# Routing logits by token rows, low parts on GpSimd, last columns in three parts, and another side for the branch to fall to

## The chip, the core and the metric

The kernel runs on one core of one Trainium2 chip, as one program. The metric is the device time of one execution in microseconds; before the change its median over three runs is 1008.89 us (1007.74 to 1009.09).

## What is computed

A two-layer block (a hybrid mixer and a convolutional feed-forward network per layer) and then a second block: a mixer and a mixture of experts. There are 256 tokens of 1024 numbers, all in fp32. The change lies in the mixture of experts, which the reference writes as

```python
glog = (t @ wg + bg).astype(f32)
gprob = jax.nn.softmax(glog, axis=-1)
g_onehot = jax.nn.one_hot(jnp.argmax(glog, axis=-1), N_GROUPS, dtype=f32)
...
elog_sel = jnp.einsum('tge,tg->te', elog, g_onehot)
eprob = jax.nn.softmax(elog_sel, axis=-1)
top_p, top_i = lax.top_k(eprob, TOP_K)
top_p = top_p / jnp.sum(top_p, axis=-1, keepdims=True)
...
for e in range(N_EXPERTS):
    hid = jax.nn.silu(t @ w_gate[e]) * (t @ w_up[e])
    y = y + gates[:, e:e + 1] * (hid @ w_down[e])
```

with 4 groups of 4 experts, the best group and its two best experts per token, and 256 hidden columns per expert.

## The kernel before, in words

The program is one long stream per engine. The layers and the second mixer take the first 860 us. `moe` (L1534) follows. Its first part, `route` (L1614), is a generator that treats the two tiles of 128 tokens, t = 0 and 1, one behind the other: it adds the out-projection to the residual rows `x` (L1620), transposes the rows on TensorE into `xr`, splits the rows into a high part `xsh` (cast on ScalarE) and a low part `xsl` (subtraction on VectorE, `split` at L362 and `low` at L354), multiplies with the router's weights `rw` (L1636, logits by columns, in fp32), copies the 20 x 128 logits and transposes them back (L1638, L1640), scales them into `rlog` (L1641), and picks group and experts with one-hot vectors (`onehot`, L1521) until `mem` (L1653) holds the membership. A product with a triangular matrix gives each token's place among the expert's tokens (`pos`, L1665 and L1666), a comparison the selection matrix `sel` (`choose`, L1591), and products with it gather the rows of the experts (`gather`, L1595, products at L1600). `low` cuts the subtraction into PIECES = 4 pieces when its engine is GpSimd. `shares` (L1673), another generator, computes the softmax weights `whl` beside it. A `Weave` (L199) interleaves the generators by the costs that they yield; the framework's scheduler then settles each engine's order from priorities and its own estimate of time.

The experts run as 8 pairs. A pair's up product (`up`, L1731) and down product (`down`, L1761) are fp32 products of 64 slots, two experts at a time in the two halves of TensorE's array (`turn`, L580, keeps their order; products at L583). `flip` (L1753, transposition at L327) turns the hidden rows; the down product is split into `yh` and `yl`, and `scatter` (L1777, products at L1783, additions on VectorE at L1784) brings two pairs at a time back to the rows `x`. Weights come through `fetch` (L1585) on SyncE in tiles of 512 KB into a ring of buffers (`er`, `ew`, `mh`, `ml`, `hres`, `grow`). The last pair is scattered alone, and each finished half of the rows is sent out (L1786) by SyncE and ScalarE.

At the end `values_load` (L1850) reads on every engine whether an expert has more than 64 tokens, and `tc.If` (L1852) runs `rest` (L1826) in that case. With these inputs it is not run. The program's blocks stand in the order kernel, `rest`, other side, end; the other side holds waits alone.

Of the kernel before, what the change touches and what calls it, by code (L numbers as in the profile page):

```python
# [10 lines left out]
F32 = mybir.dt.float32  # L11
# [6 lines left out]
P = 128  # L18
# [230 lines left out]
def emit(ctx, tc, A, out, stop=None, dbg=None):  # L249
# [76 lines left out]
    def tr(o, i):  # L326
        T.transpose(o, i, ident[:i.shape[0], :i.shape[0]])  # L327
# [1193 lines left out]
    def onehot(o, v, idx):  # L1521

        n = v.shape[1]
        m = tmp([P, n], tag="ohm")
        k = tmp([P, n], tag="ohk")
        V.tensor_reduce(m, v, axis=AX.X, op=OP.max)
# [7 lines left out]
    def moe(held, a):  # L1534
# [56 lines left out]
        def choose(t, es, src):  # L1591
            V.tensor_tensor(sel[:, t, es], io1[:, None, :].to_broadcast([P, es.stop - es.start, C]),
                            src[:, es, None].to_broadcast([P, es.stop - es.start, C]), op=OP.is_equal)

# [15 lines left out]

        got = []
        greatest = {}

        def route():  # L1614
            for t in range(NT):
# [15 lines left out]
                r = rsqrt1(ss, 1.0 / D, rows[:, t:t + 1])  # L1631
                split(xsh[:, t], xsl[:, t], x[:, t, :])
                yield (0.9, 0.8)
                p = bank(t)
                for k in range(KT):
                    T.matmul(p[:20, 128:256], rw[:, k, :], xr[:, k, :], start=k == 0, stop=k == KT - 1)  # L1636
                lT = tmp([20, 128], tag="dg")
                (V.tensor_copy if t == 0 else SC.copy)(lT, p[:20, 128:256])  # L1638
                yield (0.9, 0.2)
                tr(p[:, 0:20], lT)  # L1640
                V.scalar_tensor_tensor(rl[:, t], p[:, 0:20], r, small[:, SM_RB:SM_RB + 20], op0=OP.mult, op1=OP.add)  # L1641
# [24 lines left out]
                V.tensor_tensor(pos[:, t], pp, m, op=OP.mult)  # L1666
                choose(t, slice(0, 4), pos[:, t])
                yield (0.3, 0.8)
                if t == 1:
                    gather(0, got, range(KT), 1)  # L1670
                    yield (1.9, 0.1)

        def shares(t):  # L1673

            yield lambda: ("mem", t) in done
            m, z, den = (tmp([P, 1], tag=tag) for tag in ("smx", "smz", "smd"))
# [9 lines left out]
            V.tensor_tensor(z, z, r, op=OP.mult)  # L1686
            yield (0, 1.0)
            V.tensor_tensor_reduce(eo[:, 0], o[:, 0], ep[:, 0], 1.0, 0.0, op0=OP.mult, op1=OP.add, accum_out=den)
# [71 lines left out]

        def down(ah, cuts=(0, 1)):  # L1761
            ys = [bank(4), bank(5)]
            last = None
            ws = [[queue.pop(0) for _ in range(2)] for _ in range(2)]
            yh, yl = (tmp([P, D], F32R, tag=tag, bufs=2) for tag in ("yh", "yl"))
            steps = [(j, n) for j in range(2) for n in range(2)] if cuts else [(j, n) for n in range(2) for j in range(2)]
            for j, n in steps:
                ns = slice(n * 512, (n + 1) * 512)
                for i in range(2):
                    last = turn(last, ys[n][halves[i]], ah[:, j, halves[i]], ws[j][i][:, ns], start=j == 0, stop=j == 1)  # L1770
# [5 lines left out]

        def scatter(gys, banks, last=False):  # L1777
            rows_of = [(q, y) for q, yy in gys for y in yy]
            for i, (n, t) in enumerate((n, t) for n in range(2) for t in range(NT)):
# [4 lines left out]
                V.tensor_tensor(x[:, t, ns], p, x[:, t, ns], op=OP.add)  # L1784
                if last:
                    (nc.scalar if t else nc.sync).dma_start(out[t][:, ns], x[:, t, ns])  # L1786

# [10 lines left out]
        def experts():  # L1798
# [23 lines left out]
            scatter(ys, (3, 6, 7))  # L1822
            ys[:] = [(PAIRS - 1, down(state.pop("ah"), ()))]
            scatter(ys, (0, 1, 2, 3), last=True)

# [15 lines left out]
        for t in range(NT):  # L1841
# [9 lines left out]
                              skip_runtime_bounds_check_because="it is a comparison's 0 or 1")  # L1851
        with tc.If(full > 0):  # L1852
            rest()
# [65 lines left out]
```

## Time and profile before

| | us |
|---|---|
| median of three runs | 1008.89 |
| the profiled execution, its own time | 1010.54 |
| the profiled execution, its span | 1008.7 |
| TensorE (PE) busy | 978.6 (97%) |
| VectorE (DVE) busy | 767.1 (76%) |
| ScalarE (ACT) busy | 538.4 (53%) |
| GpSimd (POOL) busy | 115.2 (11%) |

The granted clock of TensorE is 0.987 of full speed over the span. Times in the rows below count in microseconds from the start of the span. SP is SyncE, which issues most transfers; PEld is TensorE's weight load, and a q behind an engine's name is its sequencer. Ends of matmuls are modelled, so starts are the safer numbers.

### The profile page before, as it was taken

To read this page: it belongs to the slowest core of one execution; us is meant where nothing else is said; L and a number is where in the kernel's file an instruction comes from. 1 tells how busy PE (TensorE), PEld (TensorE's weight loads), DVE (VectorE), ACT (ScalarE), POOL (GpSimd) and SP (SyncE) were. 2 spreads that over 40 slices of the span, in tenths; PEclk is the share of its full clock that TensorE was granted. 3 is DMA by queue.
4 is the path that set the end of the run, shared out by engine and by line. 5 is a ranking of instruction groups with operands and counts; after the bars stand their busy time and mean duration, and the time that the engine had idled before them with its cause. 6 is when DMAs were issued, how large, how long until landed. Compare 5 with 4: busy or idle time off the path is not lost.

```text
span 1008.7 us, 16824 instructions
## 1 busy us (share of the span) xinstructions
PE 978.6 (97%) x6056; PEld 797.8 (79%) x6056; DVE 767.1 (76%) x2004; ACT 538.4 (53%) x1036; POOL 115.2 (11%) x195
## 2 busy tenths in 40 slices
PE   8999999999999999999999999999999799899996
PEld 7888887899999988878888999999888577644432
DVE  6698688798888887986887888888899987612224
ACT  6565346766655576653457665555776434231211
POOL 1510003300000065100024000000510120000000
PEclk9999999999999999999999999999999799999998
DMA  9733025655556546330156555555553116889961
GB/s 337 248 102 105 22 84 167 230 189 179 176 188 188 188 149 206 102 111 22 56 174 230 188 173 184 188 187 187 183 177 125 63 62 245 335 322 408 408 245 45
DMA packets 51966, 181.07 MB, mean 180 GB/s; under 512 B 6274, under 2 KB 7203, under 8 KB 51875
## 3 DMA queue, kind: packets, MB, share of 16 engines
q1 hardware_dynamic: 51298, 179.33, 51.8%
q8 instruction: 49, 0.80, 0.3%
q10 hardware_dynamic: 576, 0.59, 0.2%
q14 instruction: 43, 0.34, 0.1%
HBM read 178.86 MB, written 1.05 MB: 178 GB/s over the span
## 4 chain that ended last, share of the span: by engine, by line
PE 85%; DVE 9%; issue 3%; ACT 2%; POOL 1%; DMA 0%; DVEq 0%; ACTq 0%; POOLq 0%
PE b L413 20%; PE b L414 19%; PE b L415 19%; PE b L583 11%; PE b L327 3%; PE b L901 2%; PE b L876 2%; DVE yc L1259 2%; PE b L1600 2%; PE b L1783 2%; PE b L935 1%; DVE wl L360 1%; PE b L855 1%; DVE cy L744 1%; ACT half L424 1%
## 5 line engine op out<-in xcount | busy, mean ns | idle before, releaser
L391 ACT CAST wh<-wr 128x1024 fp32r<-128x1024 f32 x233 | 243.9, 1050 | 181.7 <-PE b L414 92.0
L360 DVE TENSOR_TENSOR wl<-wr,wh 128x1024 fp32r<-128x1024 f32 x214 | 261.7, 1225 | 59.4 <-ACT wh L391 56.6
L413 PE MATMUL b<-xh,wh 128*128 128x256 f32 x816 | 234.8, 288 | 0.0
L414 PE MATMUL b<-xl,wh 128*128 128x256 f32 x816 | 232.7, 285 | 0.0
L415 PE MATMUL b<-xh,wl 128*128 128x256 f32 x816 | 232.0, 284 | 0.0
L413 PEld LDWEIGHTS b<-xh,wh 128*128 128x128 f32 x816 | 156.2, 191 | 3.5 <-issue 1.6
L414 PEld LDWEIGHTS b<-xl,wh 128*128 128x128 f32 x816 | 156.4, 192 | 1.3
L415 PEld LDWEIGHTS b<-xh,wl 128*128 128x128 f32 x816 | 156.3, 191 | 0.1
L360 POOL TENSOR_TENSOR wl<-wr,wh 128x256 fp32r<-128x256 f32 x80 | 56.8, 749 | 556.6 <-ACT wh L391 550.2
L413 PE MATMUL b<-wh,mh 128*128 128x512 f32 x272 | 108.2, 398 | 0.5 <-ACT mh L364 0.5
L414 PE MATMUL b<-wl,mh 128*128 128x512 f32 x272 | 106.8, 393 | 0.0
L413 PE MATMUL b<-wh,xh 128*128 128x512 f32 x256 | 104.3, 413 | 2.6 <-ACT xh L367 2.6
L415 PE MATMUL b<-wh,ml 128*128 128x512 f32 x272 | 106.3, 392 | 0.0
L415 PE MATMUL b<-wh,xl 128*128 128x512 f32 x256 | 104.0, 407 | 0.0
L414 PE MATMUL b<-wl,xh 128*128 128x512 f32 x256 | 103.0, 402 | 0.4 <-DVE wl L360 0.4
L1093 DVE SCALAR_TENSOR_TENSOR fu<-fq,par,fu 128x255 f32<-128x255 f32 (+1 forms) x144 | 69.0, 479 | 2.1
L413 PEld LDWEIGHTS b<-wh,xh 128*128 128x128 f32 x256 | 49.0, 192 | 14.6 <-ACT xh L367 3.8
L415 PEld LDWEIGHTS b<-wh,ml 128*128 128x128 f32 x272 | 51.1, 188 | 11.2
L413 PEld LDWEIGHTS b<-wh,mh 128*128 128x128 f32 x272 | 51.2, 188 | 10.5 <-ACT mh L364 0.8
L414 PEld LDWEIGHTS b<-wl,mh 128*128 128x128 f32 x272 | 51.3, 189 | 9.1
L415 PEld LDWEIGHTS b<-wh,xl 128*128 128x128 f32 x256 | 48.8, 191 | 11.9 <-DVE xl L368 1.2
L414 PEld LDWEIGHTS b<-wl,xh 128*128 128x128 f32 x256 | 49.2, 192 | 10.0 <-DVE wl L360 0.8
(418 smaller groups left out, 1548.3 us busy)
## 6 DMA issues: line engine op xcount, KB each, us to landing
wr<-in_win SPq DMA_DIRECT2D x78, 512.0 KB, 4.3
wr<-in_up SPq DMA_DIRECT2D x72, 512.0 KB, 3.6
wr<-in_down SPq DMA_DIRECT2D x44, 512.0 KB, 3.5
ew<-in_egu SPq DMA_DIRECT2D x30, 512.0 KB, 9.6
wr<-in_wout SPq DMA_DIRECT2D x24, 512.0 KB, 3.5
er<-in_egu SPq DMA_DIRECT2D x20, 512.0 KB, 9.7
ew<-in_edn SPq DMA_DIRECT2D x18, 512.0 KB, 10.2
wr<-in_uptok SPq DMA_DIRECT2D x16, 512.0 KB, 4.1
```

Of the source, the lines that this page charges most:

```text
L327: T.transpose(o, i, ident[:i.shape[0], :i.shape[0]])
L360: eng.tensor_tensor(l[..., c], src[..., c], h[..., c].bitcast(F32), op=OP.subtract)
L391: heads[:] = [(V.tensor_copy if first else SC.copy)(h, raw).ins]
L413: T.matmul(o, ah, bh, start=start, stop=False)
L414: T.matmul(o, ah, bl, start=False, stop=False)
L415: T.matmul(o, al, bh, start=False, stop=stop)
L583: return T.matmul(o, w, m, **kw).ins
L876: T.matmul(pq[:, u * 64:(u + 1) * 64], atu[:, u, 0, :], tv[:, u, :, 0, :], start=True, stop=True)
L901: T.matmul(pq[:, 256 + u * 64:256 + (u + 1) * 64], RRu[:, u, :], pn[:, u, :], start=True, stop=True)
L1093: V.scalar_tensor_tensor(u[:, d:], p[:, :S - d], cw[:, 2 - d:3 - d], u[:, d:], op0=OP.mult, op1=OP.add)
L1259: V.scalar_tensor_tensor(y, zp[:, ct, j:j + S], cwh[:, 31 * ct + j:31 * ct + j + 1], y, op0=OP.mult, op1=OP.add)
L1600: T.matmul(p, src[:, t, k * 128:(k + 1) * 128], sel[:, t, 4 * r:4 * r + 4, :].rearrange("p e s -> p (e s)"), start=t == 0 and n == 0 and i ...
```

## The change

Six edits. The temporaries of `onehot` get six buffers each. The low parts of the routed rows go to GpSimd. The logits are computed with the rows as the stationary operand, 128 tokens by 20 columns, so that the copy and the transposition disappear. `shares` waits for the selection of tile 1 and is issued behind its comparison. The last pair's down product has a function of its own, `down_last`, with columns in parts of 512, 256 and 256 and six output transfers for four; the two narrow parts are copied whole and scattered in fp32. The branch gets the other side as the one that it falls through to.

```diff
--- before.py
+++ after.py
@@ -1521,8 +1521,8 @@
     def onehot(o, v, idx):
 
         n = v.shape[1]
-        m = tmp([P, n], tag="ohm")
-        k = tmp([P, n], tag="ohk")
+        m = tmp([P, n], tag="ohm", bufs=6)
+        k = tmp([P, n], tag="ohk", bufs=6)
         V.tensor_reduce(m, v, axis=AX.X, op=OP.max)
         for t in range(n):
             V.scalar_tensor_tensor(o[:, t], v[:, t], m[:, t:t + 1], idx, op0=OP.is_equal, op1=OP.mult)
@@ -1589,8 +1589,8 @@
                 nc.sync.dma_start(queue[-1], todo.pop(0))
 
         def choose(t, es, src):
-            V.tensor_tensor(sel[:, t, es], io1[:, None, :].to_broadcast([P, es.stop - es.start, C]),
-                            src[:, es, None].to_broadcast([P, es.stop - es.start, C]), op=OP.is_equal)
+            return V.tensor_tensor(sel[:, t, es], io1[:, None, :].to_broadcast([P, es.stop - es.start, C]),
+                            src[:, es, None].to_broadcast([P, es.stop - es.start, C]), op=OP.is_equal).ins
 
         def gather(r, ps, ks, t):
 
@@ -1609,6 +1609,7 @@
                     SC.activation(xg[:, k], src, AF.Identity, scale=gain[:, k:k + 1])
 
         got = []
+        chosen = []
         greatest = {}
 
         def route():
@@ -1629,15 +1630,12 @@
                         tr(p[:, k4 * 128:(k4 + 1) * 128], x[:, t, k * 128:(k + 1) * 128])
                     (SC.copy if kb else V.tensor_copy)(xr[:, kb * 4:kb * 4 + 4], p.rearrange("p (k s) -> p k s", k=4))
                 r = rsqrt1(ss, 1.0 / D, rows[:, t:t + 1])
-                split(xsh[:, t], xsl[:, t], x[:, t, :])
+                split(xsh[:, t], xsl[:, t], x[:, t, :], eng=G)
                 yield (0.9, 0.8)
                 p = bank(t)
                 for k in range(KT):
-                    T.matmul(p[:20, 128:256], rw[:, k, :], xr[:, k, :], start=k == 0, stop=k == KT - 1)
-                lT = tmp([20, 128], tag="dg")
-                (V.tensor_copy if t == 0 else SC.copy)(lT, p[:20, 128:256])
-                yield (0.9, 0.2)
-                tr(p[:, 0:20], lT)
+                    T.matmul(p[:, 0:20], xr[:, k, :], rw[:, k, :], start=k == 0, stop=k == KT - 1)
+                yield (1.7, 0)
                 V.scalar_tensor_tensor(rl[:, t], p[:, 0:20], r, small[:, SM_RB:SM_RB + 20], op0=OP.mult, op1=OP.add)
                 greatest["g", t] = onehot(goh[:, t:t + 1], rl[:, t:t + 1, 0:4], idx)
                 n = [P, 1, 4]
@@ -1664,15 +1662,21 @@
                 m = mem[:, t].rearrange("p g e -> p (g e)")
                 T.matmul(pp, le, m, start=t == 0, stop=True)
                 V.tensor_tensor(pos[:, t], pp, m, op=OP.mult)
-                choose(t, slice(0, 4), pos[:, t])
+                chosen[:] = [choose(t, slice(0, 4), pos[:, t])]
                 yield (0.3, 0.8)
+                if t == 1:
+                    done.add("sel")
                 if t == 1:
                     gather(0, got, range(KT), 1)
                     yield (1.9, 0.1)
 
         def shares(t):
 
-            yield lambda: ("mem", t) in done
+            yield lambda: "sel" in done
+            with tc.issue_after(chosen[-1]):
+                share_of(t)
+
+        def share_of(t):
             m, z, den = (tmp([P, 1], tag=tag) for tag in ("smx", "smz", "smd"))
             e4, ep, eo = (tmp([P, 1, 4], tag=tag) for tag in ("e4", "ep", "eo"))
             r = rows[:, t:t + 1]
@@ -1684,7 +1688,6 @@
             SC.activation(ep[:, 0], el[:, 0], AF.Exp, bias=m2)
             V.reciprocal(z, z)
             V.tensor_tensor(z, z, r, op=OP.mult)
-            yield (0, 1.0)
             V.tensor_tensor_reduce(eo[:, 0], o[:, 0], ep[:, 0], 1.0, 0.0, op0=OP.mult, op1=OP.add, accum_out=den)
             V.reciprocal(den, den)
             V.tensor_scalar(eo, eo, den, z, op0=OP.mult, op1=OP.mult)
@@ -1758,13 +1761,12 @@
             SC.copy(ah, pt[:, 0:256].rearrange("p (j s) -> p j s", j=2))
             return ah
 
-        def down(ah, cuts=(0, 1)):
+        def down(ah):
             ys = [bank(4), bank(5)]
             last = None
             ws = [[queue.pop(0) for _ in range(2)] for _ in range(2)]
             yh, yl = (tmp([P, D], F32R, tag=tag, bufs=2) for tag in ("yh", "yl"))
-            steps = [(j, n) for j in range(2) for n in range(2)] if cuts else [(j, n) for n in range(2) for j in range(2)]
-            for j, n in steps:
+            for j, n in [(j, n) for j in range(2) for n in range(2)]:
                 ns = slice(n * 512, (n + 1) * 512)
                 for i in range(2):
                     last = turn(last, ys[n][halves[i]], ah[:, j, halves[i]], ws[j][i][:, ns], start=j == 0, stop=j == 1)
@@ -1774,7 +1776,7 @@
                 split(yh[:, ns], yl[:, ns], ys[n])
             return yh, yl
 
-        def scatter(gys, banks, last=False):
+        def scatter(gys, banks):
             rows_of = [(q, y) for q, yy in gys for y in yy]
             for i, (n, t) in enumerate((n, t) for n in range(2) for t in range(NT)):
                 ns = slice(n * 512, (n + 1) * 512)
@@ -1782,8 +1784,35 @@
                 for m, (q, y) in enumerate(rows_of):
                     T.matmul(p, selT[:, q, t * 128:(t + 1) * 128], y[:, ns], start=m == 0, stop=m == len(rows_of) - 1)
                 V.tensor_tensor(x[:, t, ns], p, x[:, t, ns], op=OP.add)
-                if last:
-                    (nc.scalar if t else nc.sync).dma_start(out[t][:, ns], x[:, t, ns])
+
+        def down_last(ah):
+
+            q = PAIRS - 1
+            ws = [[queue.pop(0) for _ in range(2)] for _ in range(2)]
+            fetch(4)
+            last = None
+            parts_of = []
+            for b, c0, c1 in ((4, 0, 512), (5, 512, 768), (2, 768, 1024)):
+                y = bank(b)[:, :c1 - c0]
+                for j in range(2):
+                    for i in range(2):
+                        last = turn(last, y[halves[i]], ah[:, j, halves[i]], ws[j][i][:, c0:c1], start=j == 0, stop=j == 1)
+                if c0 == 0:
+                    yy = tuple(tmp([P, c1 - c0], F32R, tag=tag, bufs=2) for tag in ("yh", "yl"))
+                    split(*yy, y)
+                else:
+                    yy = (tmp([P, c1 - c0], tag="yh" if b == 5 else "yl", bufs=2),)
+                    (V.tensor_copy if b == 5 else SC.copy)(yy[0], y)
+                parts_of.append((c0, c1, yy))
+            banks = [0, 1, 3, 6, 7, 0]
+            for c0, c1, yy in parts_of:
+                for t in range(NT):
+                    p = bank(banks.pop(0))[:, :c1 - c0]
+                    w = selT[:, q, t * 128:(t + 1) * 128]
+                    for m, y in enumerate(yy):
+                        T.matmul(p, w if len(yy) == 2 else w.bitcast(F32), y, start=m == 0, stop=m == len(yy) - 1)
+                    V.tensor_tensor(x[:, t, c0:c1], p, x[:, t, c0:c1], op=OP.add)
+                    (nc.scalar if t else nc.sync).dma_start(out[t][:, c0:c1], x[:, t, c0:c1])
 
         def next_rows(r, b, ks):
             def f():
@@ -1820,8 +1849,7 @@
                 state["hd"] = hd
             turned(PAIRS)()
             scatter(ys, (3, 6, 7))
-            ys[:] = [(PAIRS - 1, down(state.pop("ah"), ()))]
-            scatter(ys, (0, 1, 2, 3), last=True)
+            down_last(state.pop("ah"))
 
         def rest():
 
@@ -1849,7 +1877,7 @@
         experts()
         full = nc.values_load(overi[0:1, 0:1], min_val=0, max_val=1,
                               skip_runtime_bounds_check_because="it is a comparison's 0 or 1")
-        with tc.If(full > 0):
+        with tc.If(full > 0, preferred_fallthrough_block=False):
             rest()
 
     def store():
```

The change moves instructions on several engines. On VectorE, in the routing, where the first logits come in (`rlog` are the logits, `ohm`, `ohk` and `goh` the one-hot steps, `rs` the row norms of the other tile, `xl` the low part of tile 1, `smx` a step of the shares), before:

```order
L1630 COPY xr_10186<-b_2001_10187 128x512 [waits PE_49]
L1641 SCALAR_TENSOR_TENSOR rlog_9992<-b_1977_10115,rv_9993,small 128x20 [waits PE_49]
L346 TENSOR_SCALAR rs_2003_10199<-rs_2003_10199 128x1 [waits DVE_49]
L1526 TENSOR_REDUCE ohm_10128<-rlog_9992 128x1 [waits DVE_49]
L360 TENSOR_TENSOR xl_9991<-x,xh_9990 128x1024 [waits Activation_49]
L1528 SCALAR_TENSOR_TENSOR goh_9994<-rlog_9992,ohm_10128,cst 128x4 [waits DVE_49]
L1680 TENSOR_SCALAR smx_10156<-ohm_10128 128x1
L347 TENSOR_SCALAR rs_2003_10199<-rs_2003_10199 128x1
L1529 TENSOR_REDUCE ohk_10129<-goh_9994 128x1 [waits DVE_49]
```

and in the change:

```order
L1639 SCALAR_TENSOR_TENSOR rlog_9992<-b_1977_10118,rv_9993,small 128x20 [waits DVE_49,PE_49]
L1631 COPY xr_10166<-b_1993_10167 128x512 [waits DVE_49,PE_49,Activation_49]
L1526 TENSOR_REDUCE ohm_10128<-rlog_9992 128x1 [waits DVE_49]
L343 TENSOR_SCALAR rs_1995_10179<-ss_10159 128x1 [waits Activation_49]
L1528 SCALAR_TENSOR_TENSOR goh_9994<-rlog_9992,ohm_10128,cst 128x4 [waits DVE_49]
L344 TENSOR_SCALAR rs_1995_10179<-rs_1995_10179 128x1 [waits DVE_49]
L1529 TENSOR_REDUCE ohk_10129<-goh_9994 128x1 [waits DVE_49]
L345 TENSOR_SCALAR rs_1995_10179<-rs_1995_10179 128x1 [waits DVE_49]
L1531 TENSOR_SCALAR goh_9994<-cst,ohk_10129 128x4 [waits DVE_49]
```

The logits stand ahead of the copy `xr` instead of behind it, and the low part `xl` and the share steps are gone from between the one-hot steps.

On TensorE, at the start of the last up product (pair 7, weights `mh`, `ml`, `hres`, `grow`; `hd` are hidden rows that are transposed, `yh` and `yl` the rows that are scattered), before:

```order
L583 MATMUL b_2180_10966<-mh_10824,xg_10755 64x512 [waits DMAHW5_49]
L583 MATMUL b_2180_10966<-mh_10824,xg_10755 64x512 [waits DMAHW6_49]
L583 MATMUL b_2180_10966<-mh_10824,xg_10755 64x512 x2
L583 MATMUL b_2180_10966<-ml_10827,xg_10755 64x512 [waits DMAHW7_49]
L583 MATMUL b_2180_10966<-ml_10827,xg_10755 64x512 [waits DMAHW0_49]
L583 MATMUL b_2180_10966<-ml_10827,xg_10755 64x512 x2
L327 MATMUL b_2181_10975<-cst,hd_10948 128x128 [waits DVE_49]
L327 MATMUL b_2181_10975<-cst,hd_10948 128x128
L583 MATMUL b_2180_10966<-hres_10839,xg_10755 64x512 [waits DMAHW1_49]
L583 MATMUL b_2180_10966<-grow_10841,xg_10755 64x512 [waits DMAHW2_49]
```

and further on

```order
L583 MATMUL b_2189_11016<-er_10860,ah_10978 64x512 [waits DMAHW5_49,Activation_49]
L583 MATMUL b_2189_11016<-er_10862,ah_10978 64x512 [waits DMAHW6_49]
L583 MATMUL b_2190_11017<-er_10860,ah_10978 64x512 [waits PE_49]
L583 MATMUL b_2190_11017<-er_10862,ah_10978 64x512
L583 MATMUL b_2189_11016<-er_10868,ah_10978 64x512 [waits DMAHW7_49]
L327 MATMUL b_2193_11032<-cst,hd_10990 128x128 [waits DVE_49,PE_49]
L327 MATMUL b_2193_11032<-cst,hd_10990 128x128
L583 MATMUL b_2189_11016<-er_10870,ah_10978 64x512 [waits DMAHW0_49]
```

and in the change:

```order
L583 MATMUL b_2178_10966<-mh_10824,xg_10755 64x512 [waits DMAHW5_49]
L1785 MATMUL b_2183_10992<-yh_10902,selT_10002 128x512
L1785 MATMUL b_2183_10992<-yl_10903,selT_10002 128x512
L1785 MATMUL b_2183_10992<-yh_10952,selT_10002 128x512 [waits Activation_49]
L583 MATMUL b_2178_10966<-mh_10824,xg_10755 64x512 [waits DMAHW6_49]
L583 MATMUL b_2178_10966<-mh_10824,xg_10755 64x512 x2
L1785 MATMUL b_2183_10992<-yl_10953,selT_10002 128x512 [waits DVE_49]
L1785 MATMUL b_2184_10998<-yh_10902,selT_10002 128x512
L1785 MATMUL b_2184_10998<-yl_10903,selT_10002 128x512
```

and further on

```order
L583 MATMUL b_2178_10966<-grow_10841,xg_10755 64x512
L583 MATMUL b_2178_10966<-er_10847,xg_10755 64x512 [waits DMAHW3_49]
L583 MATMUL b_2178_10966<-er_10849,xg_10755 64x512 [waits DMAHW4_49]
L583 MATMUL b_2178_10966<-er_10847,xg_10755 64x512
L583 MATMUL b_2178_10966<-er_10849,xg_10755 64x512
L583 MATMUL b_2187_11016<-er_10860,ah_10978 64x512 [waits DMAHW5_49,Activation_49]
L327 MATMUL b_2191_11032<-cst,hd_10990 128x128 [waits DVE_49]
L327 MATMUL b_2191_11032<-cst,hd_10990 128x128
```

The first scatter products stand behind one product of `mh` instead of behind all of `mh`, `ml` and `hres`, and the transposition of `hd_10990` stands right behind the up product and one more half product, where before scatter products and five half products stood between.

On SyncE, at the end of the program (`out_dram` are the outputs, line 1852 is 1880 in the change), before:

```order
L1786 DMA out_dram<-x 128x512 [waits DMAHW5_49,DVE_49]
L1786 DMA out_dram<-x 128x512 [waits DMAHW7_49,DVE_49]
L1850 TENSOR_LOAD overi_10329 [waits DMAHW1_49,DMAHW2_49,DMAHW0_49,DMAHW3_49,DVE_49,DMAHW4_49,PE_49,DMAHW7_49,Activation_49,Pool_49]
L1852 COMPARE_AND_BRANCH
L1589 DMA ew_11101<-in_egu 128x1024 [waits DMAHW1_49,PE_49]
```

and in the change:

```order
L1815 DMA out_dram<-x 128x512 [waits DMAHW5_49,DVE_49]
L1815 DMA out_dram<-x 128x256 [waits DMAHW7_49,DVE_49]
L1815 DMA out_dram<-x 128x256 [waits DMAHW1_49,DVE_49]
L1878 TENSOR_LOAD overi_10329 [waits DMAHW1_49,DMAHW2_49,DMAHW0_49,DMAHW3_49,DVE_49,DMAHW4_49,PE_49,DMAHW7_49,Activation_49,Pool_49]
L1880 COMPARE_AND_BRANCH
L1880 UNCONDITIONAL_BRANCH [waits DMAHW0_49,DMAHW1_49,DMAHW2_49,DMAHW3_49,DMAHW4_49,DMAHW5_49,DMAHW6_49,DMAHW7_49]
```

Before, what follows the compare in the program is the spill-over pass; in the change it is a jump that waits for all queues of transfers.

## Rows read from the trace of the kernel before

**Rows 1.** The page's chain that ended last, shares of the span by engine.

```profile
PE 85%; DVE 9%; issue 3%; ACT 2%; POOL 1%; DMA 0%; DVEq 0%; ACTq 0%; POOLq 0%
```

**Rows 2.** Busy time by stretch: length, PE, PEld, DVE, ACT, POOL, PEclk, DMA, GB/s.

```profile
865.50:868.30 2.80, 0.06 (x2) 0.02 (x1) 2.73 (x27) 0.88 (x4) 0.00 (x0) 1.00 1.03 411
870.00:873.00 3.00, 3.00 (x16) 3.00 (x16) 2.58 (x15) 0.30 (x1) 0.00 (x0) 0.50 1.02 408
...
976.00:1001.00 25.00, 24.55 (x91) 9.57 (x88) 9.22 (x15) 3.56 (x7) 0.00 (x0) 1.00 0.00 1
```

**Rows 3.** Chain of waits, 854 to 880: start us, us, what.

```profile
862.99 0.14 DVE rlog L1641
...
863.33 1.13 DVE xl L360
...
866.08 0.13 DVE sm L1683
...
868.14 0.10 DVE mem L1653
...
869.56 4.58 PE b L1600 x24
...
875.05 2.10 PE b L1600 x16
877.15 3.15 PE b L583 x13
```

**Rows 4.** Instructions of line 360: count, duration ns min/median/max, first and last start.

```profile
L360 POOL TENSOR_TENSOR wl<-wr,wh x80: 719/739/1029, 163.4 to 728.4; 128x256 fp32r<-128x256 f32 x80
L360 DVE TENSOR_TENSOR ml<-fu,mh x44: 415/418/818, 209.7 to 711.0; 128x256 fp32r<-128x256 f32 x44
```

**Rows 5.** Timeline near 354.8: start us, us, engine, line, operation.

```profile
354.66 2.31 POOL L360 TENSOR_TENSOR wl<-wr,wh 128x256 fp32r<-128x256 f32 x3 [163.16 <-ACT wh L391]
...
354.86 0.82 DVE L360 TENSOR_TENSOR ml<-fu,mh 128x256 fp32r<-128x256 f32 x1 [0.51 <-ACT mh L364]
```

**Rows 6.** Timeline of PE, expert phase; each L583 product leaves two records.

```profile
980.42 1.07 PE L583 MATMUL b<-er,xg 128*64 128x512 f32 x2
981.42 0.50 PE L1783 MATMUL b<-yl,selT 128*128 128x512 f32 x1
...
982.32 1.93 PE L583 MATMUL b<-er,xg 128*64 128x512 f32 x6
984.18 0.50 PE L1783 MATMUL b<-yh,selT 128*128 128x512 f32 x1
```

**Rows 7.** Timelines of ACT and DVE, pair 7's hidden rows.

```profile
984.29 0.47 ACT L1748 ACTIVATE sg<-b,gs 128x256 f32<-128x256 f32 x1 [6.09 <-PE b L583]
...
985.56 0.48 DVE L1750 SCALAR_TENSOR_TENSOR hd<-b,share,sg 128x256 f32<-128x256 f32 x1
```

**Rows 8.** DVE's last additions (timeline), and the output transfers of line 1786.

```profile
1000.60 1.96 DVE L1784 TENSOR_TENSOR x<-b,x 128x512 f32<-128x512 f32 x3
...
L1786 ACTq DMA_DIRECT2D out_dram<-x x2: 350/356/362, 1001.3 to 1002.6; - x2
...
DMA to landing us min/median/max: 2.0/3.2/4.2
```

**Rows 9.** Instructions of line 1852, the branch.

```profile
L1852 SPq EVENT_SEMAPHORE  x8: 17/17/17, 1006.8 to 1007.4; - x8
...
L1852 PEldq COMPARE_BRANCH  x1: 4258/4258/4258, 1001.9 to 1001.9; - x1
...
L1852 SPq COMPARE_BRANCH  x1: 45/45/45, 1003.5 to 1003.5; - x1
L1852 ACTq COMPARE_BRANCH  x1: 54/54/54, 1004.2 to 1004.2; - x1
...
L1852 ACTq EVENT_SEMAPHORE  x1: 17/17/17, 1006.9 to 1006.9; - x1
```

**Rows 10.** Instructions of line 1915, the end of the program.

```profile
L1915 SPq EVENT_SEMAPHORE  x10: 17/28/28, 1007.4 to 1008.7; - x10
```

## The prediction

> **What bounds the kernel now.** I read the chain over the whole span first: 85% of it is TensorE (PE) and 9% VectorE (DVE) [rows 1]. So a microsecond saved on another engine counts only where PE waits. The change touches three such places, all behind the last out-projection.
>
> The first is the routing. The table by stretches [rows 2] shows PE busy for 0.06 of 2.80 us between 865.5 and 868.3; DVE is busy for 2.73 of them. The chain there [rows 3] is a string of small DVE operations from the logits of token tile 0 (862.99) to its membership (868.14 + 0.10), then 24 gather products (4.58 us), a wait, and 16 more (2.10 us) before the experts begin at 877.15. During 870 to 873 the granted clock is 0.50 of full speed, the lower of the two levels, after PE had been idle.
>
> The second is the end of the expert phase. From 976 on DMA moves nothing (share 0.00), and PE is busy for 24.55 of 25.00 us [rows 2]: there the order of PE's own instructions is the time. The weights are there, so the expert phase slides with its start.
>
> The third is the end: four output transfers, then the branch over the spill-over pass. On PE the compare is recorded with 4.26 us; SP compares at 1003.5 and runs its next instruction at 1006.8, ACT at 1004.2 and 1006.9 [rows 9]. From 1007.4 to 1008.7 stands the closing barrier [rows 10].
>
> About 0.2% (2.0 us) is what a measurement of this kernel can tell from no change.
>
> **Routing, DVE.** The low parts of tile 1 (1.13 us on the chain, [rows 3]) go to GpSimd (POOL). Five small share operations leave the stretch between logits and membership; the one at 866.08 costs 0.13, so all five 0 to 0.65; I take 0.25, since several fill gaps between dependent operations. Together -1.4. The logits by token rows lose a copy and a transposition, but the order still puts the copy of tile 1's transposed rows ahead of the first maximum, so that earlier logits wait there; I cost this at 0. The larger number of one-hot buffers removes no wait that the trace shows: 0.
>
> **What takes some of it back.** POOL's four pieces for tile 1, 0.74 us each in the median [rows 4], start when ACT has cast the high part, about 864.5 by an estimate from the copy and cast ahead of it, and so run until about 867.5, beside exactly this DVE chain. Where that occurred earlier in the program, a DVE subtraction that needs 418 ns in the median took 818 [rows 4]: it began at 354.86, 0.20 us into a POOL piece that began at 354.66 [rows 5]. Each collision costs DVE 0.40. Four pieces give 0 to 1.6; about seven of the DVE operations there have two inputs in SBUF, but each is short, so I take two, +0.8. The Trainium skill, in "SBUF — State Buffer", section "SBUF: two separate sides", says that a DVE operation with two SBUF inputs and a GpSimd operation that reads SBUF hold a shared pair of ports in turn, each for its whole instruction; the 818 ns agree, and by that rule alone every piece could cost up to its own length.
>
> **Routing, PE.** Tile 1's position product stands now behind 24 gather products and in the change behind 20, and the other four fill part of the gap ahead of the last 16. At 4.58/24 = 0.19 each that is -0.76. The overflow count's product and reduction now stand between position and selection: +0.15 (as the DVE operations above). -0.6. Bounds for the whole routing: -2.0 (no collision) to 0 (four); taken -1.4 + 0.8 - 0.6 = **-1.2**. The four exponentials and the remaining share work now lie beside the second gather (2.10 us); if they outlast it, the column parts of the gathered rows that DVE copies come late, and PE has two 0.86 us pairs of work before it needs them. Cost 0.
>
> **Expert phase.** Up to pair 5 PE's order is the same. Then the scatter of pairs 5 and 6 is cut into the up product of pair 7 differently. Three half-array fp32 products, in two pair times, hold PE from 982.32 until the next kind starts at 984.18; a single one, from 980.42 until 981.42; three scatter products, from 981.42 to 982.32 [rows 6]. So n pair times cost 0.86 n + 0.14, a single half costs a whole one, and m scatter products cost 0.23 m + 0.21. I counted pair times from the weights "mh" of pair 7 until the first column part of the last down product: 17 before, 18 after, since runs of 1, 3, 1, 3, 1 split pairs: +0.86. There are also two more turns from one kind of product to the other and back, 0.14 + 0.21 each: +0.7. Lastly the transposition of pair 7's hidden rows used to stand behind ten scatter products; in the change it stands right behind the up product, with one half product that shares the array with the last half. It must wait for ACT's silu (0.47, begun 0.2 after PE's end) and DVE's product (0.48) [rows 7]: 0.2 + 0.47 + 0.48 + 0.1, less the usual 0.1, is +1.15 of idle PE. Bounds: 0.9 (single halves overlap, and half the wait is filled) to 2.9; taken **+2.7**.
>
> **Last columns.** Behind the first column part DVE now does six operations on 512 columns (two low parts, four additions), at 1.96/3 = 0.65 each [rows 8]. In the change it has one low part, two additions of 512, a copy and four additions of 256, 5.5 such units: -0.33, and the last transfer is half as large. Bounds -1.0 to +0.2 (two more transfers); taken **-0.4**.
>
> **The branch.** The compare is not taken any more, but the block that it falls into ends with a jump over the whole spill-over pass, as far as the jump before. On PE, DVE and ACT it lies at the same time. On SP it stands behind eight waits for all DMA queues, so behind the landing of the output. Now SP's 3.3 us beside that landing hide it; then they add up. The last transfer is issued at 1002.6 and lands 3.2 us later in the median [rows 8]: 1005.8. The jump takes 2.7 (ACT's, the shortest seen) and the barrier 1.3 [rows 9, 10]: 1009.8 against 1008.7, **+1.1**. Bounds: landing 2.0 and a free jump, -0.8 with the jump at 2.0 and -2.8 without one; landing 4.2 and PE's 4.26, +3.7.
>
> **Sum.** -1.2 + 2.7 - 0.4 + 1.1 = +2.2 us. It is made against the profiled execution, 1010.54 us with a span of 1008.7, which is 1.65 above the median of 1008.89; on the median it gives **1011.1 us**.
>
> **Rivals.** *The far jump costs nothing.* Place: SP behind its eight waits. If what follows an unconditional jump is already there when the waits end, the program ends at 1005.8 + 1.3 = 1007.1, 1.6 earlier than now, and the sum is -1.2 + 2.7 - 0.4 - 1.6 = -0.5: 1008.4, not slower. It decides when the jump takes under 1.6 us. For it: the block that holds the waits is now reached without a jump, and SP waits there for 2 us in which something could be fetched. Against it: all three far jumps on record cost 2.7 to 4.3 us [rows 9]. The Trainium skill gives about 51 ns for a branch that is always taken ("Advanced Engine Details and Errata", section "Control Flow Timing"), which would make this rival true; "Runtime: NRT & Kernel Launch", section "Instruction fetch mechanics", says that a taken branch out of the fetched window must wait for a transfer, with which the recorded stalls agree. 0.2.
>
> *The gather keeps its clock.* The idle stretch of PE shrinks by about 0.6 us; if the clock then does not fall, 3.00 us at 0.50 [rows 2] become 1.5: 2.2 - 1.5 = +0.7, 1009.6. Against it: an idle stretch of over 2 us remains. 0.15.
>
> *PE's order at the end is harmless.* If single half products overlap with the scatter and the hidden rows come in time, the +2.7 are 0.5, and the sum is 0: 1008.9. Against it: the single product of [rows 6]. 0.15.
>
> *The low parts never get to run beside DVE*, because POOL is held up: they are first read by the gather some 5 us after POOL could be ready, so nothing changes but the collisions; it is inside the bounds.
>
> **Numbers.** The forecast has 0.5. Its own range is 1009.3 to 1013.0, from the bounds of routing, tail and landing, so that it is slower by over 2.0 us (1010.9) in about three of four such outcomes, 0.4; the rest is within. The three rivals, 0.5 together, land within 0.2% alone; two of them together, or one with the routing at -2.0, fall below 1006.9: 0.2; a sixth of them with the high landing is slower, 0.05. So faster 0.2, the same 0.35, slower 0.45. The range is 1006.2 to 1012.8: below is left the free jump with another rival, above four collisions with the longest jump.
>
> **What would show it.** Right: membership of tile 0 near 867.5 instead of 868.1, some DVE operations of two inputs twice as long; the experts' first product near 876; PE idle for about 1 us ahead of the transposition of pair 7's hidden rows; the first column part of the last down product some 1.5 us later than now; on SP the waits first, then about 3 us of nothing, then the barrier. Wrong: PE without idle time behind pair 7's up product, a barrier that follows the waits at once, or a granted clock near 1.00 throughout the gather.

## The result, and the profile after

Over 13 runs each the changed kernel took 1016.41 us in the median against 1009.62, a ratio of 1.0067 with a 95% interval of 1.0042 to 1.0091: slower by 4.2 to 9.2 us, above the range. Both kernels have executions some 6 to 8 us longer than the rest, and the profiled one of the change (1021.5 us, span 1019.6) is among them, with the clock at half between 815 and 828, ahead of everything that the change touches, so its rows are read from the first logits product on.

From there the time divides as follows, in us. The bounds are the starts of the first logits product and of the experts' first product, the end of VectorE's last addition and the end of the span: 859.75, 877.08, 1002.56 and 1008.75 before, 865.56, 882.67, 1010.34 and 1019.64 in the change. The row of the other execution is from the run under "The change again".

| | first logits product to experts | experts to the last addition | last addition to the end | sum against before |
|---|---|---|---|---|
| before | 17.33 | 125.48 | 6.19 | |
| the change | 17.11 | 127.67 | 9.30 | +5.1 |
| the change, another execution | 17.03 | 127.67 | 8.93 | +4.6 |
| forecast | -1.2 | +2.3 | +1.1 | +2.2 |

So the middle came as forecast, the routing gained 0.2 to 0.3 where 1.2 was due, and the end lost 2.7 to 3.1 where 1.1 was expected.

**Routing.** Busy time by stretch of the kernel before (columns as in [rows 2]), from 3.0 us behind its first logits product; the last stretch ends where the experts begin:

```profile
862.75:869.75 7.00, 3.43 (x27) 2.50 (x26) 6.75 (x51) 2.23 (x9) 0.00 (x0) 1.00 1.03 410
869.75:873.25 3.50, 3.50 (x18) 3.50 (x18) 2.83 (x15) 0.30 (x1) 0.00 (x0) 0.51 1.03 410
873.25:877.15 3.90, 3.24 (x30) 2.97 (x30) 2.43 (x10) 0.83 (x3) 0.00 (x0) 1.00 0.71 280
```

and of the change, from its first logits product:

```profile
865.56:868.56 3.00, 2.77 (x25) 2.53 (x23) 1.70 (x4) 1.58 (x5) 0.00 (x0) 1.00 1.03 411
868.56:879.06 10.50, 8.30 (x40) 8.06 (x41) 8.42 (x49) 1.59 (x3) 2.77 (x4) 0.53 1.02 407
879.06:882.67 3.61, 3.59 (x29) 3.21 (x28) 2.84 (x22) 1.65 (x8) 0.00 (x0) 0.96 0.28 111
```

Before, the clock is at half for some 3.5 us around the first gather, behind the stretch of [rows 2] in which PE was idle. In the change it falls 3.6 us behind the first logits product, while tile 1's logits run and though PE had been busy for 2.77 of the first 3.00 us, and is back only ten us later.

The membership of tile 0 comes little earlier. The first maximum and the membership, before:

```profile
863.17 0.15 DVE L1526 TENSOR_REDUCE ohm<-rlog 128x1 f32<-128x4 f32 x1
...
868.06 0.17 DVE L1653 TENSOR_TENSOR mem<-goh,o 128x16 f32<-128x16 f32 x1
```

and in the change:

```profile
868.60 0.15 DVE L1526 TENSOR_REDUCE ohm<-rlog 128x1 f32<-128x4 f32 x1
...
873.54 0.17 DVE L1651 TENSOR_TENSOR mem<-goh,o 128x16 f32<-128x16 f32 x1
```

Behind the first logits product, the first maximum comes at 3.04 for 3.42 us and the membership at 7.98 for 8.31. So the logits by token rows gained 0.4, and between the two nothing was gained: 4.94 for 4.89 us, though the subtraction is gone. POOL's row in the changed kernel's timeline,

```profile
870.03 2.77 POOL L360 TENSOR_TENSOR xl<-x,xh 128x256 fp32r<-128x256 f32 x4 [5.35 <-DVE rs L349]
```

lies beside these rows of DVE:

```profile
870.17 0.60 DVE L1528 SCALAR_TENSOR_TENSOR o<-el,ohm,cst 128x4 f32<-128x4 f32 x1
...
870.82 0.14 DVE L1529 TENSOR_REDUCE ohk<-o 128x1 f32<-128x4 f32 x1
...
871.06 0.40 DVE L1531 TENSOR_SCALAR o<-cst,ohk 128x4 f32<-128x4 f32 x1
...
871.50 0.64 DVE L1648 SCALAR_TENSOR_TENSOR e<-o,el 128x4 f32<-128x4 f32 x1
```

The reduction, with one input, takes its usual 0.14. The other three take 0.60, 0.40 and 0.64 where the same forms take 0.16 to 0.23 in the kernel before. With a fourth at 872.40 (0.42), the excess is 1.2 us, which gives back the 1.13 of [rows 3]. All four end within 0.02 us of the end of one of POOL's pieces, which the trace has at 870.76, 871.44, 872.12 and 872.80.

**Experts.** PE's timeline of the change, pair 7's up product (the scatter that is cut into it is that of pairs 4 and 5, which the prediction calls 5 and 6; pairs 6 and 7 are scattered alone):

```profile
979.85 1.07 PE L583 MATMUL b<-mh,xg 128*64 128x512 f32 x2
980.86 0.50 PE L1785 MATMUL b<-yh,selT 128*128 128x512 f32 x1
...
981.75 1.93 PE L583 MATMUL b<-mh,xg 128*64 128x512 f32 x6
983.61 0.50 PE L1785 MATMUL b<-yl,selT 128*128 128x512 f32 x1
...
989.14 1.07 PE L583 MATMUL b<-hres,xg 128*64 128x512 f32 x2
990.14 0.50 PE L1785 MATMUL b<-yh,selT 128*128 128x512 f32 x1
...
996.00 0.44 PE L327 MATMUL b<-cst,hd 128*128 128x128 f32 x2 [1.08 <-DVE hd L1753]
```

The single half product at 979.85 holds PE until 980.86, the one at 989.14 until 990.14, as the one in [rows 6]. The last row is the transposition of pair 7's hidden rows: PE waited 1.08 us for DVE, where 1.15 was worked out.

**End.** The branch in the change (line 1880; [rows 9] answers to it), its output transfers and the closing barrier:

```profile
L1880 SPq EVENT_SEMAPHORE  x8: 17/17/17, 1012.3 to 1015.0; - x8
...
L1880 PEldq COMPARE_BRANCH  x2: 95/2216/4338, 1009.9 to 1010.2; - x2
...
L1880 SPq COMPARE_BRANCH  x2: 43/46/49, 1011.7 to 1015.0; - x2
L1880 ACTq COMPARE_BRANCH  x2: 38/46/53, 1012.0 to 1012.2; - x2
...
L1880 ACTq EVENT_SEMAPHORE  x1: 17/17/17, 1012.1 to 1012.1; - x1
```

```profile
L1815 SPq DMA_DIRECT2D out_dram<-x x3: 332/344/348, 1008.4 to 1010.0; - x3
L1815 ACTq DMA_DIRECT2D out_dram<-x x3: 339/350/363, 1009.0 to 1010.4; - x3
...
DMA to landing us min/median/max: 2.0/2.4/4.2
```

```profile
L1943 SPq EVENT_SEMAPHORE  x10: 17/28/28, 1018.3 to 1019.6; - x10
```

ACT goes on right behind its compare (1012.0, 1012.1): falling through costs 0.1 us. The second "compare" on each engine is the jump. SP, though, runs its eight waits from 1012.3 to 1015.0, jumps at 1015.0 and is back at 1018.3.

### The profile page after: what moved, and what is told of

Read it like the earlier page. It is cut to its first block, busy times and chain, and to the rows that moved or that the text cites. A ratio compares the mean times of both kernels' runs of the same rounds, so it can differ in the third digit from the quotient of the medians.

```text
span 1019.6 us, 16864 instructions
## 1 busy us (share of the span) xinstructions
PE 988.0 (97%) x6066; PEld 805.9 (79%) x6066; DVE 766.5 (75%) x2003; ACT 537.6 (53%) x1035; POOL 120.7 (12%) x203
## 4 chain that ended last, share of the span: by engine, by line
PE 85%; DVE 9%; issue 3%; ACT 2%; POOL 1%; DMA 0%; ACTq 0%; DVEq 0%; POOLq 0%
PE b L413 19%; PE b L414 19%; PE b L415 19%; PE b L583 12%; PE b L327 3%; PE b L901 2%; DVE yc L1259 2%; PE b L876 2%; PE b L1600 2%; PE b L1785 1%; PE b L935 1%; DVE wl L360 1%; DVE cy L744 1%; PE b L855 1%; ACT half L424 1%
```

## The experiments

**The branch.** One edit on the kernel before, and the same edit taken out of the change:

```diff
-        with tc.If(full > 0):
+        with tc.If(full > 0, preferred_fallthrough_block=False):
```

> The kernel before with the branch's other side alone. The late jump on SyncE (it stands behind the landing of the output, then some 3 us of fetch): 2.5 to 3.5 us slower than before, with SyncE's eight waits ahead of the stall. The rival, that the branch costs little and the loss lies in the routing or the tail: within 1 us.

Measured: ratio 1.0038 (1.0014 to 1.0063). By the trace, routing 17.36 and experts 125.49 are those of before, and the end takes 9.06 for 6.19: +2.9.

```profile
L1852 SPq EVENT_SEMAPHORE  x8: 17/17/17, 1004.2 to 1004.7; - x8
...
L1852 PEldq COMPARE_BRANCH  x2: 95/2024/3953, 999.2 to 999.5; - x2
...
L1852 SPq COMPARE_BRANCH  x2: 43/46/49, 1000.8 to 1004.7; - x2
...
L1852 ACTq EVENT_SEMAPHORE  x1: 17/17/17, 1001.6 to 1001.6; - x1
```

```profile
L1786 ACTq DMA_DIRECT2D out_dram<-x x2: 351/356/362, 998.7 to 999.9; - x2
...
DMA to landing us min/median/max: 2.0/3.1/4.2
```

```profile
L1915 SPq EVENT_SEMAPHORE  x10: 17/28/28, 1007.6 to 1008.9; - x10
```

This is the pure case. The last transfer is issued at 999.9. SP compares at 1000.8 and its first wait ends at 1004.2, 4.2 us behind that issue, which is the longest landing. The other seven waits take until 1004.7, the jump until 1007.6 (2.9, against 3.3 in the change, in both behind the landing of the output), the barrier 1.3. In the kernel before, SP's first wait ends at 1006.8 [rows 9], and there too the last transfer lands 4.2 us behind its issue at 1002.6 [rows 8]: landing and jump end together, so a jump behind the landing adds its whole length.

> The whole change with the branch as before. The late jump: 2.5 to 3.5 us less than the change, so about 2 to 3.5 us slower than before (tail order +2.7, last columns -0.5, routing 0 to +1). The rival: as slow as the change, 5 to 6 us over before.

Measured: ratio 1.0036 (1.0010 to 1.0063), stages 16.82, 127.65 and 6.27: the end is back at that of before, and the remaining loss is the expert phase's.

**The order on PE.** The change, with the products of the scatter tied:

```diff
-                    T.matmul(p, selT[:, q, t * 128:(t + 1) * 128], y[:, ns], start=m == 0, stop=m == len(rows_of) - 1)
+                    with tc.issue_after(after) if after is not None else ExitStack():
+                        end = T.matmul(p, selT[:, q, t * 128:(t + 1) * 128], y[:, ns], start=m == 0, stop=m == len(rows_of) - 1).ins
...
-                        scatter(ys, (3, 6, 7))
+                        end = scatter(ys, (3, 6, 7), after=ups[0] if q == PAIRS - 1 else None)
...
-                    ys.append((q - 1, down(state.pop("ah"))))
+                    ys.append((q - 1, down(state.pop("ah"), last=end if q == PAIRS - 1 else None)))
```

(`ups[0]` is the last product of the up product, `last` the one that the down product's first follows.)

> The whole change, with the scatter of pairs 4 and 5 tied behind the last up product and the next down product behind the scatter. Single half products and turns between the two kinds of product cost what was counted: three pair times of 0.86, four turns of 0.35 and the 1.1 us wait for the hidden rows go, 5.1 us less than the change, so about 0.5 us around the kernel before. The rival, that the order is harmless and TensorE waits for others anyway: less than 1 us from the change.

Measured: ratio 0.9997 (0.9974 to 1.0021). The expert phase takes 122.13 for 127.67, -5.5 where 5.1 was counted, and the other stages stay (17.10, 9.57): the count of pair times, turns and the wait holds. The tied order is worth more than any other part of the change, and more than the 2.7 that the change had lost, since the order before splits pairs as well.

**The last columns.** `down_last`, as in the change, alone on the kernel before; PE's order ahead of it stays. The edit's call:

```diff
-            ys[:] = [(PAIRS - 1, down(state.pop("ah"), ()))]
-            scatter(ys, (0, 1, 2, 3), last=True)
+            down_last(state.pop("ah"))
```

> The kernel before with the last columns in three parts alone; TensorE's order ahead of the last down product stays as before. Three parts shorten the end by what the changed kernel's trace shows: 0.5 us faster than before, at most 1. The rival, that two more transfers and fp32 scatter products eat it: 0 to 0.5 us slower.

Measured: ratio 1.0006 (0.9978 to 1.0035), too wide to tell. By the trace the expert phase is 124.95, -0.5, and the end 6.53, +0.3, which takes back most of it. There the landing is not what ends last: SP compares 1.35 us behind the last addition, before 0.94, and its taken jump is over at 1004.1, 0.5 behind the last landing.

**Routing, one part out.** The whole change with the logits by columns:

```diff
-                    T.matmul(p[:, 0:20], xr[:, k, :], rw[:, k, :], start=k == 0, stop=k == KT - 1)
-                yield (1.7, 0)
+                    T.matmul(p[:20, 128:256], rw[:, k, :], xr[:, k, :], start=k == 0, stop=k == KT - 1)
+                lT = tmp([20, 128], tag="dg")
+                (V.tensor_copy if t == 0 else SC.copy)(lT, p[:20, 128:256])
+                yield (0.9, 0.2)
+                tr(p[:, 0:20], lT)
```

> The whole change, but the logits by columns as before. Read in the routing, from the first logits product to the experts' first product (17.3 us before, 17.1 in the change, where the granted clock was at half speed from 3 or 6 us behind the first logits product until 14 us behind it, and before only from 10 to 13). If the products with 20 moving columns bring the clock down early: it falls at 10 us again and the stretch takes 15 to 16.5 us though the copy and transposition are back. If the clock falls early for another reason, such as the longer idle stretch: the same half-speed stretch, 17 us or more.

Measured: the experts begin 16.44 us behind the first logits product, and the clock holds 10 us, as before (busy time by stretch, columns as in [rows 2], here and in the rows of this kind below):

```profile
859.73:866.73 7.00, 3.81 (x31) 2.88 (x30) 6.66 (x39) 0.93 (x3) 2.40 (x4) 1.00 1.03 410
866.73:870.23 3.50, 3.50 (x20) 3.50 (x18) 1.63 (x9) 0.00 (x0) 0.00 (x0) 0.51 1.03 411
```

From the membership of tile 0 to the experts it takes 8.45 us, before 9.02 and in the change 9.13. So the 0.6 that the prediction took for PE's order came, and the early fall of the clock takes 0.7 back.

The narrow products alone, the same edit the other way round on the kernel before:

> The kernel before with the logits by token rows alone. If the products with 20 moving columns bring the clock down early, without the other parts of the change: the granted clock falls 3 to 6 us behind the first logits product and stays at half until the gather's end, and from there to the experts' first product it is at least as long as before, 17.3 us, though a copy and a transposition are gone. Otherwise: it falls at 10 us as before and the stretch is 0.5 to 1 us shorter.

Measured: 17.28 us, and from 3 us behind the first logits product on

```profile
860.65:871.15 10.50, 8.06 (x40) 7.81 (x41) 9.70 (x68) 3.05 (x10) 0.00 (x0) 0.54 1.03 410
```

So it is this edit that brings the clock down sooner, and neither POOL nor the shares: a copy and a transposition less, paid for at half clock. In all eight traces with this shape the clock falls 3.4 to 6.7 us behind the first logits product; in the six with logits by columns it falls at 9.8 to 10.6, or, in one of them, not at all. The edit also leaves PE idle for 0.40 us ahead of tile 1's logits, and the narrow products and that gap were not tried apart. It changes PE's order in the last up product too: the expert phase takes 126.42, 0.9 more than before.

The whole change with the low parts on VectorE:

```diff
-                split(xsh[:, t], xsl[:, t], x[:, t, :], eng=G)
+                split(xsh[:, t], xsl[:, t], x[:, t, :])
```

> The whole change, but the low parts on VectorE. In the changed kernel's trace four one-hot operations took 1.2 us longer than elsewhere while GpSimd wrote the low parts of tile 1. If that is the shared access to memory: every one-hot operation of tile 0 is back at its short time, the subtraction of 1.2 us is back, and the time from the first maximum to tile 0's membership stays within 0.4 us of the change's 4.9. The rival, that GpSimd's work costs VectorE nothing: it grows by 1.1.

Measured: every one-hot step is back at 0.15 to 0.23, and the membership of tile 0 comes 7.84 us behind the first logits product, 7.98 in the change. The 1.2 us subtraction and the collisions are worth the same; moving the work bought nothing. The experts begin at 16.56 against 17.11, but tile 1's position product stands behind 16 gather products there and behind 20 in the change, so that this difference is not the subtraction's alone.

Tile 1's low part on VectorE, but behind the first selection:

```diff
-                split(xsh[:, t], xsl[:, t], x[:, t, :], eng=G)
+                if t == 0:
+                    split(xsh[:, t], xsl[:, t], x[:, t, :], eng=G)
+                else:
+                    SC.copy(xsh[:, t], x[:, t, :])
+                    with tc.issue_after(chosen[0]):
+                        low(xsl[:, t], x[:, t, :], xsh[:, t], V)
```

> The whole change, but tile 1's low part on VectorE, tied behind the first selection of tile 0, where VectorE has time. No collision and no subtraction in the chain: from tile 0's first maximum to its membership 3.6 to 3.9 us instead of 4.9, so the first gather begins 1.1 us sooner. If the half clock behind it then sets the rest, the experts begin less than 0.6 us sooner; if the chain does, 1 us sooner.

Measured: membership 6.85 us behind the first logits product, 1.13 sooner, as the two rows show (first logits product at 859.81):

```profile
866.66 0.17 DVE L1656 TENSOR_TENSOR mem<-goh,o 128x16 f32<-128x16 f32 x1
...
868.09 1.22 DVE L360 TENSOR_TENSOR xl<-x,xh 128x1024 fp32r<-128x1024 f32 x1
```

The experts begin at 16.82, 0.3 sooner than in the change and as in the change without the branch, whose clock was down equally long. PE is the limit behind the membership, at half clock, and its order differs: tile 1's position product waits for 24 gather products again, not for 20. The stretch, and the piece of the chain that ended last:

```profile
865.81:873.31 7.50, 6.17 (x29) 6.04 (x30) 5.42 (x25) 0.00 (x0) 0.00 (x0) 0.55 1.03 406
```

```profile
868.32 5.31 PE b L1600 x24
```

The whole change with the logits by columns, with the low parts on VectorE, and with the later low part take 1.0037, 1.0038 and 1.0056 of the time before, each give or take 0.003. These ratios do not tell them apart; the stages do, in one execution each.

An attempt to hold the clock:

```diff
+                if t == 1:
+                    for _ in range(8):
+                        T.matmul(bank(7), xsh[:, 0, 0:128], xsh[:, 0, 0:512], start=True, stop=True)
                 yield (1.7, 0)
```

> The whole change with eight more products of 512 columns (their results are not used) behind tile 1's logits, where TensorE waits for VectorE. They take 1.8 us at full clock, 3.6 at half, beside VectorE's chain of some 2 us. If the idle stretch and the narrow products bring the clock down: it stays up for part of the gather, the 40 gather products take 0.5 to 3 us less and the experts begin earlier by as much, up to 1.5 us. The rival, that the clock comes down whatever PE does there: the products cost up to 1.6 us and nothing is gained.

Measured: ratio 1.0119 (1.0060 to 1.0178), experts at 19.51, +2.4. The clock falls all the same, among the added products:

```profile
863.51:873.71 10.20, 9.80 (x36) 7.42 (x37) 4.91 (x29) 0.00 (x0) 0.46 (x1) 0.50 0.91 363
```

```profile
861.69 5.86 PE L1640 MATMUL b<-xh 128*128 128x512 f32 x8
```

They take 5.86 us, where 1.8 to 3.6 had been reckoned, most of it at half speed, and end behind the membership (864.7), which they were to fill the wait for. The rival held, and at a higher price than it named; but what products of the right length would do is left open.

**The change again.**

> The change as it is, on the same chip as the two kernels with the ordered tail. By the stages of its trace (routing -0.2 to -0.5, experts +2.2, end +3.1) about 5 us slower than before; the rival, that something ahead of the routing is slower too: 6 to 8.

Measured: ratio 1.0070 (1.0047 to 1.0093), stages 17.03, 127.67 and 8.93, a sum of +4.6. The interval begins at 4.7 us, about that sum, and its middle is 7. The fastest executions of the two kernels, 1012.18 and 1007.47, are 4.7 apart as well; what the medians have beyond that is not shown by the stages, and its cause stays open.

**Versions that beat both.** The kernel before with `down_last`, the tied order as above, and pair 6's scatter in one piece, of which the diff shows the last:

```diff
-            scatter(ys, (3, 6, 7))
-            down_last(state.pop("ah"))
+            end = scatter(ys, (3, 6, 7, 0), after=ends[0])
+            down_last(state.pop("ah"), end)
```

> The kernel before with the last columns in three parts, the scatter of pairs 4 and 5 tied behind the last up product, and pair 6's scatter in one piece with four banks ahead of the last down product. By the counted pair times (14 to the first column part of the last down product instead of 17, and two runs of scatter products for five) 2.6 + 1.0 us less, and 0.2 for the parts: 3 to 4 us faster than before. If TensorE waits for VectorE in the undivided scatter: 2 to 3.

Measured: ratio 0.9966 (0.9945 to 0.9987); stages 17.40, 120.91 and 6.52. The last-but-one down product now runs undivided, its 16 records in 3.6 us:

```profile
985.96 3.65 PE L583 MATMUL b<-er,ah 128*64 128x512 f32 x16
989.54 0.44 PE L327 MATMUL b<-cst,hd 128*128 128x128 f32 x2
```

With the routing's parts that held (logits by columns, tile 0's low part on GpSimd, tile 1's on VectorE behind the first selection, the shares behind the selection) and the branch as before:

> The same with the routing's helpful parts: logits by columns, low part of tile 0 on GpSimd and of tile 1 on VectorE behind the first selection, shares queued behind the selection. Tile 0's membership 1.1 us earlier and the half-speed stretch as short as before: 0.9 to 1.8 us less than the kernel with the ordered tail alone, 4 to 5.5 us faster than before. If the gather waits for something else: the same as that kernel.

Measured: ratio 0.9955 (0.9941 to 0.9969), 4.5 us faster than before (3.1 to 5.9); stages 15.53, 120.93 and 6.38. The interval overlaps the one above, so that the gain of the routing's parts is shown by the stages alone. In the profiled execution the clock did not fall at all:

```profile
864.28:867.28 3.00, 2.07 (x16) 1.89 (x17) 2.80 (x13) 0.00 (x0) 0.00 (x0) 1.00 1.03 410
867.28:872.81 5.53, 4.53 (x36) 3.94 (x35) 4.80 (x31) 1.62 (x8) 0.00 (x0) 1.00 1.02 404
```

That is one execution; whether the clock holds in every one is open.

## Why the prediction was wrong

**The branch, +1.1, is the term that failed most.** The mechanism was right: SP's jump stands behind the landing and then adds up. Its size was not: I took the median landing (3.2 us, [rows 8]) where the last transfer decides, which lands 4.2 us behind its issue; I left out the eight waits, which take 0.5 and which the kernel before also has behind its jump, ahead of the barrier; and I took ACT's 2.7 for a jump that takes SP 2.9 here and 3.3 in the change. The branch alone costs 2.9. The first rival, a free jump, was wrong; the bounds held the value.

**Routing, -1.2, measured -0.2 to -0.3.** Of this, the part on DVE (-1.4 + 0.8) came as -0.3 and the part on PE (-0.6) as +0.1 in the profiled execution. The part on DVE failed in its second half: four collisions of 1.2 us in sum instead of two of 0.8, so that taking the subtraction off DVE gained nothing. The 0.3 is from the logits' new shape, which was costed at 0 there: luck, in the direction forecast. The part on PE assumed that the clock would do what it did before, and did not cost that shape at all. With the old shape it comes as -0.6, as reckoned; the new one, taken alone, brings the clock down 3.9 us behind its start. A rival had the clock staying up; none had it falling sooner, and none with PE busy ahead of it.

**Experts, +2.7, and the last columns, -0.4,** measured 2.2 together against 2.3. With the last columns alone the phase takes 124.95, so that the order's share is 2.7, as reckoned. The order of instructions, with the durations of single halves and turns, was enough for it; the third rival, a harmless order, fell with the tied kernel. The last columns gain 0.5 in this phase and lose 0.3 at the end, -0.2 for -0.4.

**The whole.** The terms as measured by the traces give 4.6 to 5.1 us, within the interval; the forecast's 2.2 was less than half of that. The range left out, above, the bad bounds of the routing and of the branch together, and nearly that came.

## What to carry to other kernels

Where a scheduler settles the order, look at every engine's order behind an edit, also far from it: edits in the routing cost 2.7 us in the last up product (127.67 against 124.95 with the last columns alone, and 127.65 without the branch's edit), and tying that order was worth more than the edits could be. What waits ahead of a barrier was set here by the last transfer's landing (4.2 us), not by the median, and an instruction stall that used to lie beside it adds up once it stands behind it. Moving work to an idle engine need not be free: four pieces on GpSimd held up VectorE by 1.2 us, as much as the subtraction had taken there.

## What was not expected of the hardware

A compare that is not taken costs 0.1 us (ACT 1012.0 to 1012.1), and the jump behind it as much as a taken compare did: on SP 2.9 to 3.5 us with the output already landed, for 3.0 to 3.3 of the taken compare in the kernels with the branch as before. The Trainium skill gives about 51 ns for a branch that is always taken ("Advanced Engine Details and Errata", section "Control Flow Timing"). These jumps over a long block are far from it, and the measurement decides.

Operations on four numbers per partition were held for up to 0.48 us by a neighbour of 0.72 us on GpSimd, one with a single full operand and a scalar per partition from SBUF among them (871.06). And two groups of eight products with 20 moving columns were followed, 3.4 to 6.7 us behind the first, by a granted clock of half speed, which came at 9.8 us or later with 128 columns in the same place.
